# A hybrid DeltaNet and attention trunk: its first layer begun on half the tokens, the second layer's modulation sums moved to another stage, and the attention mask taken into the scan

## The chip, the cores and the metric

One Trainium2 chip, one core of it. The metric is the device time of one execution in microseconds (us), the median of several runs. The engines are named as the profile does: PE (TensorE, the matmuls), DVE (VectorE), ACT (ScalarE), POOL (GpSimd) and SP (SyncE, whose queue issues the transfers).

## The reference

Two layers on 1024 tokens of width 1024, all in float32. Both get six vectors of 1024 values each (shift, scale and gate for the mixer and for the FFN) from one conditioning vector. Layer one's mixer is a gated DeltaNet with 8 heads, layer two's is stick-breaking attention with 16 heads of width 64; each is followed by a SwiGLU FFN of inner width 2816.

```python
def reference(x, c, ada_w, ada_b, ...):
    cond = silu(c)
    for i in range(2):
        mod = cond @ ada_w[i] + ada_b[i]                    # 6 * 1024 values
        sh1, sc1, gt1, sh2, sc2, gt2 = split(mod, 6)
        h = rms_norm(x, norm1_g[i]) * (1 + sc1) + sh1
        y = gated_deltanet_mixer(h, ...) if i == 0 else stick_breaking_mixer(h, ...)
        x = x + gt1 * y
        h = rms_norm(x, norm2_g[i]) * (1 + sc2) + sh2
        x = x + gt2 * ((silu(h @ gate_w) * (h @ up_w)) @ down_w)
    return x

# stick-breaking attention, for a block of 128 queries and all keys up to it
z = q @ k.T * scale
causal = s_pos < t_pos                                      # strictly below the diagonal
log_1m = where(causal, log_sigmoid(-z), 0)
log_stick = cumsum(log_1m, reverse=True) - log_1m
a = where(causal, exp(log_sigmoid(z) + log_stick), 0)
o = a @ v
```

## The kernel before

The activations lie transposed: x is 8 tiles of 128 features by 1024 tokens (`xs[k]`), and a half c of the tokens is 512 of them. Each large product is done as three matmuls of 128 x 512 in a reduced format (`mm3`, L269, L271, L273): the high part of the weights (`wh`) by the high part of the activations, `wh` by their low part, and the low part of the weights (`wl`) by the high part. Both weight parts are made as the weights arrive, `wh` by a cast on ACT (L263) and `wl` by a subtraction on DVE (L264); `slab` loads 128 x 512 weights and splits them. The normed input `h` is split in the same way.

There are five stages.

1. **Start.** x is loaded half after half (`load_x`). For each half ACT squares it, DVE adds the squares up (L329), PE sums over the features (`norm_scale`, L333), and DVE multiplies x by the result (L1525). Then eight blocks of 1 MB of the modulation weights are loaded (`first_mods`); PE multiplies each by the conditioning vector (L97, L101) and `place_mods` puts two columns each into `mod` (L228, L229). That is shift and scale of the first mixer. `make_gsc` (L365) and `norm_part` (L342 to L346) then make `h` for both halves.
2. **DeltaNet.** Eight heads go through stages a to d, merged round by round (`t` from -2 to 6). `stage_a(0)` computes q and k of head 0 for the first half and then for the second, then the small products for the gates a and b (L743), then v. The other 32 column blocks of layer one's modulation are spread over the rounds as units of `row_steps` on PE (L97, L101, ended by L205), by a table of counts.
3. **FFN0.** `ffn(0)` walks over 22 column blocks f. The FFN's products are arranged as a fast matrix multiplication with seven products in place of eight, so DVE has many additions (L463, L551 to L604) between them. For even f the two blocks of f before it are multiplied by the output weights (`out_gemm`). Beside it runs `side`, units of layer two's modulation (`mod_unit`): 256 KB is loaded for each half of a unit, scaled by the conditioning values, summed over 8 blocks of 128 x 128, and `mod_end` (L205) sums over the partitions on PE. 24 of the 48 units are done here, three for two values of f, in the form `spare`: ACT scales (L172) and POOL adds (L178 to L183).
4. **Attention.** `stickbreak.main` first makes the second half of h (`norm_h`), spills x to memory, and then `attention` runs head pairs: `qkv(pp + 1)` is merged with `attend(pp)` and three modulation units in the form with sums on DVE (L174 once and L176 seven times for a unit). Three units are left behind the seventh round. For a block of queries `scores` makes z for two heads on PE, sigmoids of z and of -z on ACT (L1425), a scan on DVE that multiplies the second up from right to left (L1429), and a product of both on DVE (L1431); `turned` transposes on PE (L1442) and copies on ACT (L1443), and `weigh` multiplies by v. The mask is added to z on the diagonal block by two matmuls with `mask_b` (L1421, in the trace under L97).
5. **FFN1**, the same as FFN0 without `side`.

The order on every engine's queue is fixed when the program is built: a list scheduler takes instructions in the order of the code, and `merge` interleaves generators by the costs that they yield.

## Time and profile before

| | |
|---|---|
| median of three runs | 2895.55 us (2890.51 to 2895.74) |
| the profiled execution | 2890.06 us, its span 2888.4 us |
| PE | 2716.4 us busy, 94% |
| DVE | 2033.9 us, 70% |
| ACT | 1381.7 us, 48% |
| POOL | 95.1 us, 3% |
| transfers | 214 MB, 74 GB/s over the span |

The granted clock of PE was 0.98 of full speed over the span. The stages lie at about 0 to 59 us (start), 59 to 700 (DeltaNet), 700 to 900 (output products and the first part of FFN0), 900 to 1490 (FFN0), 1490 to 2105 (attention), and 2105 to 2888 (output products and FFN1). Busy shares are averages over these stages; what an edit is worth is read from its own stage.

### The profile page before, as it was taken

How to read it: one execution, taken by the hardware profiler on the slowest of the kernel's cores; microseconds unless marked ns; L12 is line 12 of the kernel's file. 1: busy time of each engine (PE TensorE's matmuls, PEld its weight loads, DVE VectorE, ACT ScalarE, POOL GpSimd, SP SyncE). 2: the span in 40 equal slices, each digit the busy share in tenths (PEclk: the TensorE clock that was granted, in tenths of full speed). 3: DMA queues.
4: the chain of work that ended last, by engine and by line, in shares of the span. 5: the costliest groups of instructions: out<-in, count | busy, mean ns of one | idle time of the engine just before them, and what ended most of it. 6: DMA issues, size and time to landing. Idle time of an engine off the chain costs nothing.

```text
span 2888.4 us, 40153 instructions
## 1 busy us (share of the span) xinstructions
PE 2716.4 (94%) x15202; PEld 2161.4 (75%) x15202; DVE 2033.9 (70%) x3352; ACT 1381.7 (48%) x2920; POOL 95.1 (3%) x174
## 2 busy tenths in 40 slices
PE   4999999998989999999999999999898999999999
PEld 2777777776767888778877666667576788888887
DVE  5777666666696666667786777677858866667666
ACT  5455555555453333433246777777845323223232
POOL 0000000001000111110000000000000000000000
PEclk9999999998999999999999999999899999999999
DMA  6312222234112222222231111111321111111113
GB/s 218 108 56 83 80 76 72 80 103 144 59 37 70 80 70 81 70 82 78 61 110 66 51 52 52 48 52 52 132 66 55 46 57 55 52 54 49 55 56 102
DMA packets 136288, 214.22 MB, mean 74 GB/s; under 512 B 33696, under 2 KB 62240, under 8 KB 136096
## 3 DMA queue, kind: packets, MB, share of 16 engines
q1 hardware_dynamic: 136096, 211.66, 23.1%
q8 instruction: 120, 1.97, 0.3%
q14 instruction: 72, 0.59, 0.1%
HBM read 195.75 MB, written 15.86 MB: 73 GB/s over the span
## 4 chain that ended last, share of the span: by engine, by line
PE 67%; DVE 15%; ACT 12%; DMA 3%; issue 3%; POOL 1%; SPq 0%; ACTq 0%; POOLq 0%; DVEq 0%
PE m L269 9%; PE m L273 8%; PE m L271 8%; PE s L273 6%; PE s L269 6%; PE s L271 5%; PE g L273 5%; PE g L269 5%; PE g L271 5%; DVE S L1429 2%; PE m L97 2%; DMA ada<-in_ada_w_dram 2%; ACT S L1425 2%; DVE wl L264 1%; PE s L97 1%
## 5 line engine op out<-in xcount | busy, mean ns | idle before, releaser
L269 PE MATMUL m<-h,wh 128*128 128x512 f32 x904 | 360.9, 408 | 7.3 <-DVE X L371 5.1
L273 PE MATMUL m<-h,wl 128*128 128x512 f32 x904 | 350.7, 397 | 10.6 <-DVE wl L264 10.6
L271 PE MATMUL m<-h,wh 128*128 128x512 f32 x904 | 351.1, 397 | 0.3 <-DVE h L359 0.3
L269 PE MATMUL g<-h,wh 128*128 128x512 f32 x856 | 313.4, 407 | 22.8 <-ACT wh L263 20.0
L273 PE MATMUL g<-h,wl 128*128 128x512 f32 x856 | 308.4, 401 | 13.0 <-DVE wl L264 13.0
L371 DVE SCALAR_TENSOR_TENSOR X<-m,mod,X 128x512 f32<-128x512 f32 x224 | 166.8, 750 | 209.7 <-PE m L273 209.6
L271 PE MATMUL g<-h,wh 128*128 128x512 f32 x856 | 303.1, 398 | 0.8 <-DVE h L447 0.8
L263 ACT CAST wh<-ga 128x512 fp32r<-128x512 f32 x168 | 100.7, 621 | 291.6 <-PE s L271 142.1
L273 PEld LDWEIGHTS m<-h,wl 128*128 128x128 f32 x904 | 172.5, 191 | 47.6 <-DVE wl L264 12.3
L269 PEld LDWEIGHTS m<-h,wh 128*128 128x128 f32 x904 | 171.7, 190 | 47.3 <-DVE X L371 8.0
L269 PEld LDWEIGHTS g<-h,wh 128*128 128x128 f32 x856 | 157.6, 190 | 58.8 <-ACT wh L263 25.8
L273 PEld LDWEIGHTS g<-h,wl 128*128 128x128 f32 x856 | 160.4, 190 | 52.9 <-DVE wl L264 20.9
L271 PEld LDWEIGHTS m<-h,wh 128*128 128x128 f32 x904 | 172.6, 191 | 34.5 <-DVE h L359 1.4
L1429 DVE TENSOR_TENSOR_SCAN S<-S,sbc 128x256 f32<-128x256 f32 (+7 forms) x128 | 170.0, 1348 | 33.0 <-ACT S L1425 32.9
L271 PEld LDWEIGHTS g<-h,wh 128*128 128x128 f32 x856 | 160.3, 190 | 33.2 <-DVE h L447 1.1
L263 ACT CAST wh<-wr 128x512 fp32r<-128x512 f32 x170 | 105.1, 625 | 146.4 <-PE m L271 74.3
L1425 ACT ACTIVATE S<-g,rq 128x512 f32<-128x512 f32 (+5 forms) x258 | 140.7, 596 | 37.2 <-DVE X L1431 15.3
L264 DVE TENSOR_TENSOR wl<-wr,wh 128x512 fp32r<-128x512 f32 x170 | 115.7, 684 | 52.0 <-ACT wh L263 51.9
L371 DVE SCALAR_TENSOR_TENSOR X<-s,mod,X 128x512 f32<-128x512 f32 x192 | 142.8, 744 | 13.1 <-PE s L273 13.0
L273 PE MATMUL s<-E,wl 128*128 128x512 f32 x352 | 137.7, 392 | 4.2 <-DVE wl L264 4.2
L269 PE MATMUL m<-S,wh 128*128 128x512 f32 x352 | 138.5, 394 | 0.0
L269 PE MATMUL s<-E,wh 128*128 128x512 f32 x352 | 138.2, 393 | 0.0
(454 smaller groups left out, 6040.4 us busy)
## 6 DMA issues: line engine op xcount, KB each, us to landing
ada<-in_ada_w_dram SPq DMA_DIRECT2D x160, 256.0 KB, 2.6
wo<-in_ffn_wo_dram SPq DMA_DIRECT2D x96, 256.0 KB, 2.8
ua<-in_ffn_wi_dram SPq DMA_DIRECT2D x88, 256.0 KB, 2.6
ga<-in_ffn_wi_dram SPq DMA_DIRECT2D x42, 512.0 KB, 3.6
wr<-in_dn_w_dram SPq DMA_DIRECT2D x68, 256.0 KB, 2.9
wr<-in_sb_w_dram SPq DMA_DIRECT2D x54, 256.0 KB, 2.7
E<-in_ada_w_dram SPq DMA_DIRECT2D x8, 1024.0 KB, 10.1
wr<-in_dn_wo_dram SPq DMA_DIRECT2D x24, 256.0 KB, 2.6
```

What stands on the lines that cost most here:

```text
L97: ins = f()
L263: S.copy(out=hi[:, :w], in_=raw[:, :w])
L264: V.tensor_tensor(out=lo[:, :w], in0=raw[:, :w], in1=hi[:, :w].bitcast(F32), op=ALU.subtract)
L269: PE.matmul(o, lhsT=wh, rhs=mh, start=start, stop=False)
L271: PE.matmul(o, lhsT=wh, rhs=ml, start=False, stop=False)
L273: PE.matmul(o, lhsT=wl, rhs=mh, start=False, stop=stop)
L371: V.scalar_tensor_tensor(out=xs[k][:, cs], in0=ps, scalar=mod[:, layer, 24 * which + 16 + k:24 * which + 17 + k], in1=xs[k][:, cs], op0=AL ...
L1425: S.activation(out=o[hd][:, tk], in_=z[:, hd, 0:wb], func=AF.Sigmoid, scale=rq[:, c, i, hd:hd + 1])
L1429: V.tensor_tensor_scan(pw[:, 0:w][:, ::-1], pw[:, 0:w][:, ::-1], zero_b.to_broadcast((P, w)), 1.0, op0=ALU.mult, op1=ALU.add)
```

## The change

- x is loaded half by half: `fetch_x(0)`, the squares and the norm of that half, the eight blocks of `first_mods`, the first two weight slabs of q (`there`), then `fetch_x(1)`. `stage_a(0)` does q and k for the first half of the tokens, then calls `second`, which norms the second half and makes its h, and then does the second half.
- The counts of layer one's units in DeltaNet's rounds are 4 4 3 3 3 3 3 3 6 in place of 3 3 4 4 4 4 4 3 3.
- Of layer two's 48 units 40 run in FFN0 (five for two values of f) with the sums on DVE, with a single buffer for the loaded half, and 8 in attention, one in a round and one behind the seventh.
- `stickbreak.main` hands the second half's norm and the spill of x to `attention` as a generator (`second`, the letter n in the order string `od0`), and `qkv(0)` takes its steps between its products.
- The mask matmuls are gone. The scan's second operand is now a real tile `late`, 0 and, on and above the diagonal, 1, with maximum in place of addition, so that the running product is 1 there. Behind `turned` POOL sets the diagonal block of the transposed weights to zero where the mask is (64 selections of 128 x 256).

```diff
+    def slabs(src):
+        return [slab(src[:, half * HALF:(half + 1) * HALF], 4) for half in range(2)]
...
                 next(side, None)
+                next(side, None)
                 if f % 2 == 0:
...
-    def deltanet(h, after):
+    def deltanet(h, after, there, second):
...
+            if hh == 0:
+                pre = [big(), big()]
+                for c in range(2):
+                    if c:
+                        second()
+                    for i in range(2):
+                        yield from gemm_steps([pre[i][:, c, :]], [c], dn_w[i * NH + hh], h,
+                                              there=None if c or i else there)
...
-            add(islice(mg, (3, 3, 4, 4, 4, 4, 4, 3, 3)[t + 2]), 'oM')
+            add(islice(mg, (4, 4, 3, 3, 3, 3, 3, 3, 6)[t + 2]), 'oM')
...
-            run(norm_h(h, 1, 0, 1, accs[0], ("S4", "S6")))
-            spill_x()
-            attention(h, after)
+            def second():
+                for _ in norm_h(h, 1, 0, 1, accs[0], ("S4", "S2")):
+                    yield 1.0
+                spill_x()
+            attention(h, after, second())
...
+        late = cp.tile([P, T], mybir.dt.bfloat16, tag="eye16", name="late")
+        G.memset(late[:, 0:T - P], 0.0)
...
+        V.tensor_copy(late[:, T - P:], late_f)
...
-            od0 = '012a435bNNdeyTNNy'
+            od0 = '0n1nnnnnnnnnr24a35bNNdeyTNNy'
...
-                if b == nb - 1:
-                    for hd in range(2):
-                        made.append(partial(PE.matmul, z[:, hd, wb - P:wb], lhsT=ident_b, rhs=dmask, start=False,
-                                            stop=True))
...
-                V.tensor_tensor_scan(pw[:, 0:w][:, ::-1], pw[:, 0:w][:, ::-1], zero_b.to_broadcast((P, w)), 1.0,
-                                     op0=ALU.mult, op1=ALU.add)
+                V.tensor_tensor_scan(pw[:, 0:w][:, ::-1], pw[:, 0:w][:, ::-1], late[:, T - w:T][:, ::-1], 1.0,
+                                     op0=ALU.mult, op1=ALU.max)
...
+            own = aT[i // 4][:, :, i % 4, ts_]
+            G.affine_select(out=own, in_=own, pattern=[[0, 2], [1, P]], compare_op=ALU.is_gt, fill=0.0, base=0,
+                            channel_multiplier=-1)
...
-        mg = mod_steps(1, range(24, 48))
+        mg = mod_steps(1, range(40, 48))
         run(qkv(0))
         for t in range(SBP - 1):
-            merge([attend(t), qkv(t + 1), islice(mg, 3)], [56.448, 40.2, 40.5])
+            merge([attend(t), qkv(t + 1), islice(mg, 1)], [56.448, 40.2, 40.5])
...
+    fetch_x(0)
+    load_x(0, range(KT))
     for q in range(KT):
         rows.append(first_mods(0, q))
...
-        todo.append(ffn(0, mod_steps(1, range(24), spare=True)))
+        todo.append(ffn(0, mod_steps(1, range(40))))
...
+        there = slabs(dn_w[0])
+        fetch_x(1)
+        def half_h(c):
+            for k in range(KT):
+                norm_part(h, 0, 0, c, k, xs[k][:, c * HALF:(c + 1) * HALF], k % 2 == 1)
+        def second():
+            load_x(1, range(KT), ("S2", "S0"))
+            half_h(1)
```

The order on PE at the very start of the kernel before (names with numbers are buffers; `m_136` and `m_172` are the two norm sums, `E_...` the modulation blocks):

```order
L333 MATMUL m_136<-S_5_110,onesf 128x512
L333 MATMUL m_172<-S_5_110,onesf 128x512
L101 MATMUL m_187<-E_10_185,sc_c 32x256
L97 MATMUL m_187<-E_10_185,sc_c 32x256 x7
L101 MATMUL m_200<-E_13_198,sc_c 32x256
L97 MATMUL m_200<-E_13_198,sc_c 32x256 x7
L228 MATMUL s_211<-cT,row_196 128x1 x2
```

And on PE in the changed kernel, where the first half's products of q and k end (L336 is the norm sum, `adac` and `ada` belong to units of `row_steps`, L748 are the gate products, called L743 before):

```order
L271 MATMUL g_427<-h_323,wh_487 128x512
L273 MATMUL g_427<-h_315,wl_488 128x512
L336 MATMUL m_520<-S_5_110,onesf 128x512
L205 MATMUL m_593<-cT,adac_453 128x1
L101 MATMUL m_596<-ada_597,sc_c 32x128
L97 MATMUL m_596<-ada_597,sc_c 32x128 x3
L97 MATMUL m_596<-ada_599,sc_c 32x128 x4
L748 MATMUL m_653<-h_308,S_116_649 32x512
```

The second norm sum has moved from in front of the modulation products to behind the first half's q and k.

The order on DVE in FFN0 before, at the end of an even f (L588 to L604 combine the seven products; `wl_9386` and `wl_9403` are the first low weights of the next f):

```order
L588 TENSOR_TENSOR S_1622_9101<-m_9315,S_1609_9039 128x512
L589 TENSOR_TENSOR S_1609_9039<-g_9083,S_1609_9039 128x512
L463 TENSOR_TENSOR s_1683_9424<-ga_9381,ua_9420 128x512
L595 TENSOR_TENSOR S_1622_9101<-s_9335,S_1622_9101 128x512
L264 TENSOR_TENSOR wl_9386<-ga_9381,wh_9385 128x512
L596 TENSOR_TENSOR S_1622_9101<-g_9083,S_1622_9101 128x512
L597 TENSOR_TENSOR S_1609_9039<-S_1622_9101,S_1609_9039 128x512
L602 TENSOR_TENSOR S_1609_9039<-m_9355,S_1609_9039 128x512
L264 TENSOR_TENSOR wl_9403<-ga_9381,wh_9402 128x512
```

The same place on DVE in the changed kernel (`adac` and `ada` are the modulation unit; lines are three or so higher):

```order
L591 TENSOR_TENSOR S_1603_8955<-m_9007,S_1590_8893 128x512
L174 TENSOR_SCALAR adac_8990<-ada_8991,sc_c 128x128
L592 TENSOR_TENSOR S_1590_8893<-g_8937,S_1590_8893 128x512
L176 SCALAR_TENSOR_TENSOR adac_8990<-ada_8991,sc_c,adac_8990 128x128
L598 TENSOR_TENSOR S_1603_8955<-s_9027,S_1603_8955 128x512
L176 SCALAR_TENSOR_TENSOR adac_8990<-ada_8991,sc_c,adac_8990 128x128
L599 TENSOR_TENSOR S_1603_8955<-g_8937,S_1603_8955 128x512
L176 SCALAR_TENSOR_TENSOR adac_8990<-ada_8991,sc_c,adac_8990 128x128
L600 TENSOR_TENSOR S_1590_8893<-S_1603_8955,S_1590_8893 128x512
L605 TENSOR_TENSOR S_1590_8893<-m_9047,S_1590_8893 128x512
L264 TENSOR_TENSOR wl_9078<-ga_9073,wh_9077 128x512
```

Four of the unit's eight sums stand between the additions, and the next f's first `wl` has moved behind L605, the addition that takes the last product.

## Rows read from the trace of the kernel before

**Rows 1.** The page's part 4, the chain that ended last: share by engine.

```profile
PE 67%; DVE 15%; ACT 12%; DMA 3%; issue 3%; POOL 1%; SPq 0%; ACTq 0%; POOLq 0%; DVEq 0%
```

**Rows 2.** Timeline, start: us, duration, engine, line, operation, count, idle before it and releaser.

```profile
25.61 2.08 PE L333 MATMUL m<-S,onesf 128*128 128x512 f32 x2 [9.61 <-DVE S L329]
...
44.22 0.16 DVE L229 TENSOR_TENSOR mod<-s,sc_c 128x2 f32<-128x2 f32 x1 [1.02 <-PE s L228]
...
58.72 0.80 PE L269 MATMUL g<-h,wh 128*128 128x512 f32 x1 [13.97 <-ACT wh L263]
...
83.09 7.56 PE L743 MATMUL m<-h,S 128*32 128x512 f32 x32
...
92.30 0.71 PE L269 MATMUL g<-h,wh 128*128 128x512 f32 x2
```

**Rows 3.** Window: length, engines' busy us (instructions), PEclk, DMA share, GB/s.

```profile
2.00:31.50 29.50, 7.94 (x38) 2.71 (x39) 18.24 (x36) 15.34 (x26) 1.10 (x7) 1.00 0.97 357
```

**Rows 4.** Window in DeltaNet's first rounds: PE, PEld, DVE, ACT, POOL.

```profile
120.00:140.00 20.00, 15.39 (x125) 12.48 (x126) 19.58 (x42) 8.70 (x20) 0.00 (x0) 0.91 0.46 131
```

**Rows 5.** Timeline, PE: one unit of layer one's modulation among the v products.

```profile
105.26 0.28 PE L205 MATMUL m<-cT,adac 128*128 128x1 f32 x2
...
106.04 0.72 PE L269 MATMUL g<-h,wh 128*128 128x512 f32 x2
```

**Rows 6.** One line, L585 on ACT, in FFN0 and in FFN1: durations, first and last start.

```profile
L585 ACT ACTIVATE S<-S x17: 632/633/636, 868.1 to 1367.2; 128x512 f32<-128x512 f32 x17
...
L585 ACT ACTIVATE S<-S x17: 632/633/634, 2267.4 to 2749.5; 128x512 f32<-128x512 f32 x17
```

**Rows 7.** Timeline, PE: the ending of a unit in FFN0 among the products.

```profile
916.82 0.39 PE L273 MATMUL s<-E,wl 128*128 128x512 f32 x1
917.05 0.28 PE L205 MATMUL m<-one,adac 128*128 128x1 f32 x2
...
917.50 0.40 PE L271 MATMUL m<-E,wh 128*128 128x512 f32 x1
```

**Rows 8.** Window in FFN0, and from its waits: us, times, longest.

```profile
905.00:1350.00 445.00, 437.82 (x1930) 357.12 (x1929) 305.06 (x484) 171.36 (x373) 66.12 (x105) 1.00 0.25 76
...
PE g L273 <- DVE wl L264: 4.2, 8, 0.6
```

**Rows 9.** Groups by line: a modulation unit's sums on DVE (busy us, mean ns).

```profile
L176 DVE SCALAR_TENSOR_TENSOR adac<-ada,sc_c,adac 128x128 f32<-128x128 f32 x168 | 58.6, 349 | 11.3 <-DMA ada<-in_ada_w_dram 7.7
L174 DVE TENSOR_SCALAR adac<-ada,sc_c 128x128 f32<-128x128 f32 x24 | 6.6, 277 | 0.0
```

**Rows 10.** Waits in attention, 1570 to 2145 us; and its units by form.

```profile
DVE adac L176 <- DMA ada<-in_ada_w_dram: 6.0, 7, 3.5
...
L174 DVE TENSOR_SCALAR adac<-ada,sc_c 128x128 f32<-128x128 f32 x22 | 6.1, 276 | 0.0
```

**Rows 11.** Groups by form: one subtraction on DVE, FFN0 (905 to 1350), FFN1 (2300 to 2745).

```profile
L463 DVE TENSOR_TENSOR S<-S,S 128x512 fp32r<-128x512 f32 x30 | 23.2, 775 | 12.8 <-ACT S L607 12.8
...
L463 DVE TENSOR_TENSOR S<-S,S 128x512 fp32r<-128x512 f32 x31 | 21.2, 684 | 0.0
```

**Rows 12.** Timeline, PE: the second norm sum at attention's start.

```profile
1511.80 2.07 PE L333 MATMUL m<-S,onesf 128*128 128x512 f32 x2 [4.63 <-DVE S L329]
```

**Rows 13.** Window of one attention round; timeline of two mask products.

```profile
1694.49:1766.53 72.04, 66.23 (x420) 49.61 (x419) 50.71 (x76) 56.22 (x107) 0.00 (x0) 1.00 0.16 52
...
1747.37 0.28 PE L97 MATMUL g<-mask_b 128*128 128x128 bf16 x2
1747.47 0.48 PE L269 MATMUL m<-h,wh 128*128 128x512 f32 x1
```

**Rows 14.** Groups by line: a selection on POOL; the scan on DVE.

```profile
L699 POOL TENSOR_SCALAR_AFFINE_SELECT S<-S 128x128 f32<-128x128 f32 x1 | 0.3, 343 | 0.0
...
L1429 DVE TENSOR_TENSOR_SCAN S<-S,sbc 128x256 f32<-128x256 f32 (+7 forms) x128 | 170.0, 1348 | 33.0 <-ACT S L1425 32.9
```

**Rows 15.** Timeline behind the seventh round: DVE and PE.

```profile
2052.95 1.51 DVE L176 SCALAR_TENSOR_TENSOR adac<-ada,sc_c,adac 128x128 f32<-128x128 f32 x4 [3.48 <-DMA ada<-in_ada_w_dram]
...
2069.85 2.91 PE L1442 MATMUL s<-ident,X 128*128 128x128 f32 x12 [2.48 <-ACT E L1443]
```

68 lines of the change are left out of this document (33 added, 35 removed).

## The prediction

> **What bounds the kernel now.** I read the chain of work that ended last first: 67% of it is TensorE (PE), 15% VectorE (DVE) and 12% ScalarE [rows 1]; the busy shares of the table say the same. So a change can win in three ways only: fill the stretches where PE stands idle, take instructions off PE, or shorten the waits of PE. The timeline and the windows show where PE is idle: the first 58 us, the front of DeltaNet where DVE is full, small gaps in each attention round, and the end of attention. The two FFNs are the control: FFN1 runs the same products as FFN0 without any modulation beside them.
>
> **Start: x in halves (first part of the change).** Before, PE's queue holds the norm sum of the second half of x ahead of the first modulation products; it runs at 25.61 us after 9.61 us of idleness [rows 2], and only then do the eight modulation blocks follow, about 2.1 us apart, up to the last modulation on DVE at 44.22 us [rows 2]. In the change the eight 1 MB blocks are loaded right behind the first half of x. The transfers move 357 GB/s from 2 to 31.5 us [rows 3], which is 29.5 x 0.357 = 10.5 MB, just the 2.1 MB of half an x and the 8.4 MB of blocks. So the last block lands near 31.5 us. Behind a block's landing I take 2.4 us for its products, its copy and its add (one block's pitch before and a little more), which puts the last modulation at 33.9 us: 10.3 us sooner. The first product began at 58.72 us [rows 2], 14.5 us behind the modulations: it waited for the cast of its weight slab, which stood on ScalarE behind nearly all casts of both halves of h. In the order of the change that slab is cast ahead of h, so the first product can follow in 2.4 us, near 36.3 us: 22.4 us sooner. Not all of this is kept. The q and k products of the first half are 48 matmuls of 0.23 us, the pitch of such matmuls [rows 7], 11 us; I let them end near 51.5 us, four us later than that, because h comes chunk by chunk from ScalarE and PE has stood idle before. Then PE takes the second norm sum, about 2 us [rows 2], and must wait until DVE and ScalarE have made the scale and the second half of h; from the eight DVE multiplications and the first cast I allow 6 us until the first piece is there, and the rest arrives at the pace of the products. The 32 products of a and b (7.56 us) stand in the same stretch. That leads to the v products near 77 us in place of 92.30 us [rows 2], a gain of about 15 us. Behind this DVE is the bound: it is busy for 19.58 of the 20 us from 120 on, while PE is busy for 15.39 [rows 4]. DVE's own work for head 0 can begin sooner by the same time, so most of the gain passes through. I take **-13 us**, bounds -16 and -8 (half of it lost in that stretch).
>
> **Row units of layer 0.** A unit holds PE from 105.26 to 106.04 us, 0.78 us [rows 5]. Five of them go from the middle rounds, where PE is nearly full, to the first two rounds and the last, where PE has idle time. All of it gained is 5 x 0.78 = 3.9 us; some of the ends is not idle. **-2 us**, bounds -4 and -1.
>
> **FFN0.** Two values of f make a pair of steps, the period in which the products repeat. ScalarE's silu of the same kind stands at 868.1 and 1367.2 us, eight pairs apart in FFN0, and at 2267.4 and 2749.5 us in FFN1 [rows 6]: 62.39 us a pair against 60.26. FFN0 pays 2.13 us a pair for its three modulation units. One ending of a unit (L205) costs PE about 0.22 us: a matmul at 916.82 has 0.23 us to itself, while from the ending at 917.05, with one matmul behind it, it is 0.45 us to the next at 917.50 [rows 7]. Three are 0.66 us; 1.47 us is left for waits, of which the waits for wl alone are 4.2 us in 445 us [rows 8]. After it there are five units a pair: 1.10 us for the endings. The sums leave ScalarE and GpSimd and go to DVE: one scaling of 277 ns and seven multiply-adds of 349 ns [rows 9], 2.72 us a unit, 13.6 us a pair. DVE is busy for 305.06 of 445 us there [rows 8], 42.8 us a pair, so it comes to 56.4 us of some 62.8 us, 90%. That covers the work by 6.4 us a pair, and no more: the order shows the first wl of the next f now behind the addition that waits for the last product (L605), where it stood ahead of it before, so PE meets a wait of about 1 us there in each f; against that ScalarE loses 8 scalings a unit, and its casts come sooner. A unit also has one buffer of half its size, and its next half is fetched only when the four sums have ended; in attention, where this scheme runs now, DVE waits 6.0 us in all for that data, 7 times in 22 units [rows 10]. I take the waits at 1.4 us, as now: 60.26 + 1.10 + 1.4 = 62.76 us, 0.37 us a pair more, **+3 us** over eight pairs. If casts and products get easier to 0.4 us of waits it is -5 us; if each f pays 1.5 us (3.05 us a pair) it is +16 us. I stay near the middle, since rows on DVE at 90% do not exist in this trace.
>
> One row on GpSimd leaving: the subtraction of two SBUF tiles takes 775 ns in FFN0 and 684 ns in FFN1 [rows 11], 30 of them in 445 us: 0.09 x 30 / 7.1 pairs, 0.4 us of DVE a pair, which is inside the bounds.
>
> **Attention, start.** The first products no longer stand behind the whole second norm in the code. In PE's order the second norm sum comes after one product of the first half instead of before it, and PE waited 4.63 us for it [rows 12]; DVE's sums, for which it waits, are the same and DVE is full there. **-1 us**, bounds -3 and 0.
>
> **Attention, the seven rounds.** A round takes 72.04 us, PE is busy for 66.23 and DVE for 50.71 [rows 13]. Gone are 128 mask products: two of them hold PE from 1747.37 to 1747.47 us [rows 13], so 64 pairs cost 64 x 0.11 = 7 us. Gone are 16 of the 24 endings of units, 16 x 0.22 = 3.5 us, and with 14 of the 21 units of the rounds 14 x 2.72 = 38 us of DVE [rows 9]. PE's share alone is 7 + 3.5 = 10.5 us; part of it only widens the idle 5.8 us of a round, since the tails of the cycle sigmoid, scan, multiplication, transposition set the pace in a few places. New are 64 selections on GpSimd of 128 x 256 elements between the copy and the weighing products. The nearest row is a 128 x 128 one of 343 ns [rows 14]; between the same and double it is 0.34 to 0.69 us. The weighing product stands a scores step behind its last copy, so I cost them at nothing; if that cover were gone, half of the 64 (one in each pair of blocks is the late one) would cost 32 x 0.69 = 22 us at the most. The scan keeps its form and length with a true second operand for a repeated one; its rows are 170.0 us in all [rows 14]; at nothing, and at 5% either way 8.5 us of DVE, mostly idle-covered. **-8 us**, bounds -14 and +3.
>
> **Attention, end.** Three units were run behind the seventh round, at the time when DVE leads the chain: it stood 3.48 us for their data, and PE waited 2.48 us for a tile behind [rows 15]. One unit is left. **-4 us**, bounds -6 and -2.
>
> **The sum.** -13 - 2 + 3 - 1 - 8 - 4 = -25 us. The profiled execution took 2890.06 us, 5.5 us under the median of the runs shown, 2895.55. From the first it is 2865, from the second 2870.5; I take **2868 us** between them.
>
> **Rivals.** *VectorE becomes the bound in FFN0* (slower). If each of the ten half units of a pair makes DVE wait x us for its transfer, a pair takes 56.4 + 10x us: it binds from x = 0.64, and from x = 0.95 (65.9 us) the whole gain of 25 us is gone. For it: data waits of up to 3.48 us [rows 15] happen already where units stand close. Against: the mean wait per half is 6.0 / 44 = 0.14 us in attention [rows 10]. At x = 1.3 a pair takes 69.4 us, 6.6 us more than forecast, 53 us in all: 2921 us. *The start's gain is given back*: DVE, full from 120 to 140 us [rows 4], has no earlier work to take, and the wait for the second half is longer than I allow; 3 us of 13 stay: 2878 us. *The selections disturb the scans*: GpSimd's selection and DVE's scan and multiplication meet, each of the 64 holds DVE for 0.34 to 0.69 us, 64 x 0.5 = 32 us, 40% of it in the tails where DVE leads: +13 us, the body ends at +5 in place of -8: 2881 us. For it: the lengthened subtractions beside GpSimd's additions [rows 11]. Against: DVE has 21 us free in a round.
> The Trainium skill (SBUF — State Buffer, section Who interferes with whom) has this as a rule that speaks against the change: an operation of DVE with two SBUF inputs contends with a GpSimd instruction that reads SBUF, and one of them blocks for the whole instruction of the other. The trace agrees where GpSimd works, 775 against 684 ns [rows 11]; no run here shows it on a scan. By the rule in full the time would be that of the rival of the selections.
> *It moves costs about and no more*: FFN0 pays 16 us in place of 3 and the start keeps 5 of 13, with the rest as forecast less 2: 2868 + 13 + 8 + 2 = 2891 us, within 0.2% of before.
>
> **How the numbers follow.** Forecast 65%, start given back 12%, selections 10%, costs moved 6%, VectorE bound 7%. Faster by over 0.2% (5.8 us, about what can be told from no change): 65 + 12 + 10 = 87%; within 0.2%: 6%; slower: 7%. The bounds of the terms add to -48 and +8 us; all ends together are unlikely, so below I go to 2846 (-22 from the forecast), above to 2890, which takes in the start and the selections and leaves out the last two cases and a little of the low end.
>
> **What would show it.** In the changed profile: the last modulation near 34 us, the first product near 36, the v products near 77; the FFN0 silu rows 62 to 63.5 us a pair, with DVE near 90% busy; rounds of attention of about 71 us and no PE wait for GpSimd; scans of unchanged length; no DVE wait of 3 us for modulation data at the end of attention. A pair over 65 us, scans longer by a tenth, or v products behind 88 us would prove the forecast wrong.

## The result

The changed kernel takes 2907.64 us (median of seven runs), the kernel before 2894.05 us in the runs beside it: ratio 1.0055, 95% interval 1.0037 to 1.0072, some 16 us slower (13.6 us between the two medians). Forecast were 25 us less. The profiled execution has a span of 2909.1 us against 2888.4. In that execution of the kernel before, the first product comes early, at 58.72 us; in the ten later runs with the same start it comes at 59.77 to 63.53 us. Against one of those the differences in the table below would be one to five us smaller.

The page of the changed kernel, parts 1 and 4 (busy time, share and count of each engine; the chain that ended last), answers to [rows 1]:

```profile
PE 2729.1 (94%) x15074; PEld 2168.8 (75%) x15074; DVE 2086.1 (72%) x3543; ACT 1319.8 (45%) x2722; POOL 58.8 (2%) x118
...
PE 69%; DVE 17%; ACT 8%; DMA 3%; issue 3%; SPq 0%; ACTq 0%; DVEq 0%
```

PE has 128 instructions less and is busy for longer. The page doesn't say where; a list of landmarks on the timeline does. Each is the start of one instruction that both kernels have.

| landmark | before | after | difference |
|---|---|---|---|
| modulations of the first mixer ready (make_gsc) | 44.41 | 43.84 | -0.6 |
| first product | 58.72 | 45.41 | -13.3 |
| head 0's v convolution (ACT) | 105.46 | 100.80 | -4.7 |
| head 1's k convolution | 143.59 | 143.54 | 0.0 |
| head 1's v convolution | 154.29 | 157.13 | +2.8 |
| head 2's q convolution | 187.25 | 204.93 | +17.7 |
| head 7's v convolution | 613.38 | 620.81 | +7.4 |
| first output product of DeltaNet | 696.47 | 725.04 | +28.6 |
| FFN0, silu of f = 2 | 868.10 | 892.35 | +24.3 |
| FFN0, silu of f = 18 | 1367.17 | 1407.57 | +40.4 |
| attention's first scan | 1572.93 | 1616.60 | +43.7 |
| first scan of the seventh round | 2000.20 | 2026.70 | +26.5 |
| FFN1, silu of f = 2 | 2267.40 | 2289.33 | +21.9 |

So there are two losses in DeltaNet (first rounds, and between the last round and the output product) and one in FFN0, and one gain, larger than forecast, in attention's rounds. Windows in DeltaNet show idle PE (columns as in [rows 4]; the column behind the engines is the granted clock):

```profile
100.00:120.00 20.00, 14.25 (x93) 10.57 (x91) 8.95 (x16) 12.76 (x39) 0.74 (x1) 0.74 0.50 132
...
140.00:160.00 20.00, 15.42 (x72) 12.25 (x70) 18.70 (x31) 8.60 (x24) 0.52 (x1) 0.97 0.18 63
160.00:180.00 20.00, 16.22 (x173) 13.36 (x173) 9.52 (x11) 6.44 (x24) 0.74 (x1) 0.60 0.13 41
...
700.00:730.00 30.00, 16.74 (x97) 12.35 (x97) 14.83 (x35) 14.44 (x38) 0.00 (x0) 0.60 0.64 202
```

PE works 14.25 of 20, 31.64 of 40 and 16.74 of 30 us there, part of it at the lower of its two rates (granted 0.74, 0.60 and 0.60 on the mean), beside stretches in which it stood still. The first of these gaps is made up again, for head 1's k convolution is not late. The lasting loss of the first rounds lies between head 1's v and head 2's q convolution, so in the second. In the gaps from 100 and from 700 us, and behind 160 us, no engine is full, so PE waits for something in a queue. The timeline of the changed kernel gives PE's waits, and the transfer queue of SP beside them (start and duration in us, engine, line, operation; in brackets the wait ahead and what ended it):

```profile
76.35 27.62 SPq L193 DMA_DIRECT2D ada<-in_ada_w_dram  x4
...
105.02 0.39 SPq L257 DMA_DIRECT2D wr<-in_dn_w_dram  x1
...
109.68 1.22 PE L269 MATMUL g<-h,wh 128*128 128x512 f32 x2 [3.52 <-ACT wh L263]
...
138.03 7.04 SPq L193 DMA_DIRECT2D ada<-in_ada_w_dram  x3
...
155.27 0.61 PE L273 MATMUL g<-h,wl 128*128 128x512 f32 x2
160.54 0.36 PE L101 MATMUL m<-dd,S 64*64 64x64 f32 x1 [4.66 <-DVE dd L1047]
...
167.18 0.38 SPq L257 DMA_DIRECT2D wr<-in_dn_w_dram  x1
...
174.66 0.73 PE L269 MATMUL g<-h,wh 128*128 128x512 f32 x2 [1.68 <-ACT wh L263]
...
701.03 2.75 SPq L193 DMA_DIRECT2D ada<-in_ada_w_dram  x3
...
706.18 2.41 SPq L386 DMA_DIRECT2D yr<-ydn  x3
...
725.04 1.22 PE L269 MATMUL m<-h,wh 128*128 128x512 f32 x2 [2.71 <-ACT wh L263]
```

From 76 to 104 us SP's queue is in the loads of four half units of layer one's modulation (L193); the next weights of DeltaNet (L257) are issued at 105.02, and PE waits for their cast until 109.68. From 138 us more half units follow, and the next weights are asked for at 167.18. PE's last product with weights ends at 155.88, and the next comes at 174.66; between them PE has only the small products of a head, which wait for DVE, and those of a unit. At the end the last three of these loads stand at 701 to 704 us, and only at 706 come the loads of `yr`, the input of the output product. Units and weights share three buffers (`wr`). So the waits of SP's queue in the changed kernel name L97 on PE, the products of the unit before, as releaser (total us, times, longest), from 60 to 180 us:

```profile
SPq L193 <- PE m L97: 45.2, 3, 21.7
```

That gave theory A, that the added units stand ahead of the weights in SP's queue, with the halved start as its rival for the first rounds (theory B).

### The profile page after: what moved, and what is told of

Same layout as the page of the kernel before. It is cut to its first block, busy times and chain, and to the rows that moved or that the text cites. A ratio compares the mean times of both kernels' runs of the same rounds, so it can differ in the third digit from the quotient of the medians.

```text
span 2909.1 us, 39773 instructions
## 1 busy us (share of the span) xinstructions
PE 2729.1 (94%) x15074; PEld 2168.8 (75%) x15074; DVE 2086.1 (72%) x3543; ACT 1319.8 (45%) x2722; POOL 58.8 (2%) x118
## 4 chain that ended last, share of the span: by engine, by line
PE 69%; DVE 17%; ACT 8%; DMA 3%; issue 3%; SPq 0%; ACTq 0%; DVEq 0%
PE m L269 10%; PE m L273 9%; PE m L271 9%; PE s L269 5%; PE s L273 5%; PE s L271 5%; PE g L269 5%; PE g L271 5%; PE g L273 4%; PE m L97 2%; DVE wl L264 2%; PE s L1464 1%; DVE S L1451 1%; ACT S L1446 1%; PE s L97 1%
## 5 line engine op out<-in xcount | busy, mean ns | idle before, releaser
L273 PE MATMUL g<-h,wl 128*128 128x512 f32 x856 | 312.4, 403 | 17.7 <-DVE wl L264 17.5
L1451 DVE TENSOR_TENSOR_SCAN S<-S,late 128x256 f32<-128x256 f32 (+7 forms) x128 | 171.5, 1361 | 70.0 <-ACT S L1446 70.0
L263 ACT CAST wh<-wo 128x512 fp32r<-128x512 f32 x96 | 59.7, 622 | 198.4 <-PE s L271 97.3
```

Of the source, the lines that this page charges most:

```text
L263: S.copy(out=hi[:, :w], in_=raw[:, :w])
L273: PE.matmul(o, lhsT=wl, rhs=mh, start=False, stop=stop)
L1451: V.tensor_tensor_scan(pw[:, 0:w][:, ::-1], pw[:, 0:w][:, ::-1], late[:, T - w:T][:, ::-1], 1.0, op0=ALU.mult, op1=ALU.max)
```

## Experiments on DeltaNet's counts and the start

Edits are given against the kernel before, or against the changed kernel where it says so. All ratios are to runs of the kernel before beside them, whose median lay between 2894 and 2897 us.

**e1: the counts undone** (on the changed kernel).

```diff
-            add(islice(mg, (4, 4, 3, 3, 3, 3, 3, 3, 6)[t + 2]), 'oM')
+            add(islice(mg, (3, 3, 4, 4, 4, 4, 4, 3, 3)[t + 2]), 'oM')
```

> The changed kernel with one line undone: layer one's modulation units go over DeltaNet's rounds as 3 3 4 4 4 4 4 3 3 again. Theory A (queue): the four units in the first rounds and the six in the last take the three buffers that the weights use too; SP's queue stands at their loads and the next weights stand behind. That costs about 17 us by head 2's first convolution and about 21 us between the last round and the first output product, against 5 us won in the middle. Undone, the first output product comes near 695 us instead of 725, and the time falls by 25 to 33 us, to about 2880 us, below the kernel before. Theory B (halved start): the loss of the first rounds belongs to the halved start, and only the last round is cured: 17 us less and 5 us of the middle lost again, about 2895 us, with head 2's first convolution still near 205 us.

2888.4 us, ratio 0.9974 (0.9964 to 0.9984): 19 us below the changed kernel and 8 us below the one before. Head 2's q convolution comes at 187.91 us, the first output product at 698.86. Windows of e1:

```profile
100.00:120.00 20.00, 19.41 (x144) 14.56 (x143) 11.88 (x25) 14.42 (x46) 0.74 (x1) 1.00 0.49 132
120.00:140.00 20.00, 14.11 (x84) 11.08 (x84) 18.70 (x38) 6.92 (x13) 0.00 (x0) 0.74 0.51 147
...
160.00:180.00 20.00, 19.88 (x230) 16.08 (x230) 9.41 (x12) 9.09 (x30) 0.52 (x1) 1.00 0.17 53
...
700.00:730.00 30.00, 28.95 (x144) 23.50 (x143) 21.60 (x42) 16.28 (x36) 0.00 (x0) 1.00 0.45 150
```

And the timeline of e1 in the first rounds and at DeltaNet's end (start, duration, engine and line):

```profile
77.20 3.50 SPq L193 DMA_DIRECT2D ada<-in_ada_w_dram  x2
82.58 0.33 SPq L257 DMA_DIRECT2D wr<-in_dn_w_dram  x1
87.05 17.62 SPq L193 DMA_DIRECT2D ada<-in_ada_w_dram  x2
...
158.88 0.50 PE L273 MATMUL g<-h,wl 128*128 128x512 f32 x1
...
658.12 9.26 SPq L386 DMA_DIRECT2D yr<-ydn  x3
...
687.16 1.38 SPq L257 DMA_DIRECT2D wr<-in_dn_wo_dram  x2
...
698.86 0.48 PE L269 MATMUL m<-h,wh 128*128 128x512 f32 x1
```

PE is full from 160 to 180 and from 700 to 730 us at the granted clock 1.00. The gap from 100 us has only moved: from 120 to 140 us PE works 14.11 us at 0.74, so that gap is not the loss. In e1 a load of weights stands at 82.58 us between the units, and from 80 to 140 us the queue asks for weights seven times, in the changed kernel six times; so e1 still has products with weights to put between the small ones behind 157 us (158.88). At the end `yr` is asked for at 658 us in place of 706, and the output weights at 687 us, where the changed kernel asks at 721. SP's wait by itself does not tell the two apart, for from 60 to 180 us e1 has nearly as much of it:

```profile
SPq L193 <- PE m L97: 37.3, 3, 17.7
```

What counts is which loads stand behind it. Theory A holds for both places; B falls. The time gained, 19 us by the medians, is less than the 25 to 33 us expected.

**e2: the counts alone.** The one line of e1 the other way round, on the kernel before.

> The kernel before with only the counts 4 4 3 3 3 3 3 3 6. Theory A: both losses appear without any other edit, first output product near 725 us instead of 696, 25 to 33 us slower, about 2923 us. Theory B: the first rounds stay as before (head 2's first convolution near 187 us), the last round costs about 17 us and the middle gives 5: about 2906 us.

2921.67 us, ratio 1.0086 (1.0069 to 1.0103): 25 us slower without any other edit. Head 2's q convolution at 210.74 us, first output product at 728.72. Both losses are the counts'.

**e3: the halved start alone**: `fetch_x`, `there`, `second` in `deltanet` and `half_h` as in the diff, and nothing else.

> The kernel before with only the halved start (x in halves, q and k of the first half of the tokens first). Theory A: the halved start keeps the 4.7 us that it wins by head 0's last convolution (100.8 us against 105.5), about 2889 us. Theory B: it loses some 12 us in the first rounds, head 2's first convolution near 205 us instead of 187, about 2906 us. In both the modulation blocks take about 3.4 us each on PE instead of 2.15, because PE stays at its lower rate through the start.

2891.96 us, ratio 0.9981 (0.9972 to 0.9991), 5 us faster, where 13 were forecast. Head 0's v convolution comes at 100.93 us, head 2's q convolution at 187.84. The modulation blocks take 3.4 us each, as in the changed kernel.

**e9: six units at the end alone.**

```diff
-            add(islice(mg, (3, 3, 4, 4, 4, 4, 4, 3, 3)[t + 2]), 'oM')
+            add(islice(mg, (3, 3, 4, 4, 4, 3, 3, 2, 6)[t + 2]), 'oM')
```

> The kernel before with counts 3 3 4 4 4 3 3 2 6: the first rounds untouched, six units in the last. If the six units alone hold the weight buffers in front of the first output product, head 2's first convolution stays near 190 us while that product comes 18 to 22 us later than before, behind a last round otherwise equal: 15 to 20 us slower, about 2913 us. If both places need each other (the queue stays behind from the first rounds on), it is within 5 us of before.

2912.17 us, ratio 1.0051 (1.0028 to 1.0074). Head 2's convolution is not late (189.15 us), the first output product comes at 720.15. The six units cost 15 us (by the ratio) to 18 us (by the medians) by themselves; the queue need not be behind before.

## Experiments on the modulation in FFN0

The step of a pair of f values, as in [rows 6] (L588 is the silu, L585 in kernels with the old numbering), is read from the group of these silus (count, durations, first and last start). First the changed kernel:

```profile
L588 ACT ACTIVATE S<-S x17: 632/633/635, 892.4 to 1407.6; 128x512 f32<-128x512 f32 x17
```

The same group in e4:

```profile
L585 ACT ACTIVATE S<-S x17: 632/633/636, 870.8 to 1389.2; 128x512 f32<-128x512 f32 x17
```

And in e11:

```profile
L585 ACT ACTIVATE S<-S x17: 632/633/635, 871.6 to 1359.3; 128x512 f32<-128x512 f32 x17
```

An eighth of the stretch from first to last is 64.40, 64.80 and 60.96 us; before it was 62.39.

**e4: the moved modulation alone.**

```diff
+                next(side, None)
...
-        todo.append(ffn(0, mod_steps(1, range(24), spare=True)))
+        todo.append(ffn(0, mod_steps(1, range(40))))
...
-            merge([attend(t), qkv(t + 1), islice(mg, 3)], [56.448, 40.2, 40.5])
+            merge([attend(t), qkv(t + 1), islice(mg, 1)], [56.448, 40.2, 40.5])
```

> The kernel before with only layer two's modulation moved: 40 units in FFN0 with sums on VectorE, 8 in attention. If the units themselves make FFN0 slower, the pair of steps takes 64.4 us as in the changed kernel (62.4 before), 16 us in all; attention's rounds shrink from 72.0 us to 70.5 to 71, 7 to 10 us in all, its end by 3 us: about 2897 to 2900 us. If the cost of FFN0 came from somewhere else in the change, the pair stays near 62.7 us and the time is about 2886 us.

2902.38 us, ratio 1.0024 (1.0014 to 1.0033): 7 us slower, near the first value expected. FFN0 loses 19 us by this edit alone; five rounds of attention take 358.98 us against 362.07, 0.6 us a round.

**e10: forty units in the old form** (on e4).

```diff
-        todo.append(ffn(0, mod_steps(1, range(40))))
+        todo.append(ffn(0, mod_steps(1, range(40), spare=True)))
```

> The kernel before with 40 units in FFN0 and 8 in attention, but FFN0's in the old form: ScalarE scales, GpSimd adds. VectorE keeps its old load there. If VectorE's load makes FFN0 slower, the pair of steps takes 62.4 + 2 x 0.22 = 62.8 us; if the number of units does it (the one buffer, the transfers in the queue, the endings), it takes 64 us or more also here.

2960.46 us, ratio 1.0225 (1.0195 to 1.0255); the pair takes 71.2 us. That is the side of the number of units in what was expected, but it does not show them as the cause in e4: this form itself does not carry five units, and PE waits 25.3 us in 425 us for casts on ScalarE, which now stand among the scalings.

**e11: the old 24 units, summed on VectorE.**

```diff
-        todo.append(ffn(0, mod_steps(1, range(24), spare=True)))
+        todo.append(ffn(0, mod_steps(1, range(24))))
```

> The kernel before with the same 24 units in FFN0 and 24 in attention, but FFN0's sums on VectorE instead of ScalarE and GpSimd. If VectorE's load is the cause, the pair of steps takes between 62.4 and 64.4 us, near 63.3 by its share (three fifths); if ScalarE's and GpSimd's work was the hindrance before, it falls below 62.

2877.91 us, ratio 0.9942 (0.9919 to 0.9964), 17 us faster than before by one argument. A window of 425 us in FFN0, of e11:

```profile
915.00:1340.00 425.00, 425.00 (x1895) 352.24 (x1894) 340.17 (x641) 117.77 (x197) 0.00 (x0) 1.00 0.26 79
```

The same window of e4:

```profile
915.00:1340.00 425.00, 407.62 (x1792) 330.00 (x1792) 343.22 (x715) 109.75 (x183) 0.00 (x0) 1.00 0.29 90
```

With 24 units PE has no idle time at all; the pair is FFN1's 60.26 us and three endings, 0.66. With 40, at nearly the same busy time of DVE (343 against 340 us, 81% where 90% was forecast), PE stands 17.4 us. DVE's mean load does not tell the two apart, and the old form on ScalarE and GpSimd was itself the hindrance before. Among PE's waits in e4 is the one that the prediction named (total us, times, longest):

```profile
PE g L273 <- DVE wl L264: 11.8, 7, 1.7
```

**e13: that wait taken away.** On e4, the split of each f's first weights gets a high priority, so that its low part stands ahead of the closing additions.

```diff
-            product(b1, ga[:, 0], b11)
+            product(b1, ga[:, 0], b11, True)
...
+            if early:
+                with tc.high_priority():
+                    hi, lo = split_slab(w, HALF)
```

> Forty units in FFN0 as in the run with the moved modulation alone (2902 us, pair of steps 64.8 us), but the split of each f's first weights gets a high priority, so that its low part stands ahead of the closing additions of the f before on VectorE's queue, as it does with 24 units. Theory O (order): the two us a pair are PE's wait for that low part behind the additions; the pair falls to 61.5 to 62.3 us and the time to 2880 to 2885 us. Theory L (load): VectorE is too full with 40 units, whatever the order; the pair stays at 64 us or more and the time within 5 us of 2902.

2908.54 us, ratio 1.0045 (1.0031 to 1.0059), pair 64.9 us. The wait is gone (1.3 us in 420 us) and others stand in its place: for the unit's sums before an ending (3.3 us), for casts on ScalarE (2.4 us). They are smaller: PE stands 9.4 us in 420 where it stood 17.4 in 425, and yet the pair is no shorter, since PE is busy for longer in each; why is open. Theory O falls.

**e14: 32 units**, two in an odd f, two in an even one; 16 in attention.

```diff
                 next(side, None)
+                if f % 2:
+                    next(side, None)
...
-            merge([attend(t), qkv(t + 1), islice(mg, 3)], [56.448, 40.2, 40.5])
+            merge([attend(t), qkv(t + 1), islice(mg, 2)], [56.448, 40.2, 40.5])
...
-        todo.append(ffn(0, mod_steps(1, range(24), spare=True)))
+        todo.append(ffn(0, mod_steps(1, range(32))))
```

> 32 units in FFN0 (four a pair of steps) on VectorE and 16 in attention. In its order the next f's first low weights stand behind the additions in every second f, as with 40 units. Theory O: the stall is nearly that of 40 units, pair 63.5 to 64.5 us. Theory L: the load lies halfway between 24 (60.96 us) and 40 units (64.8 us), pair near 62 us, or lower still where VectorE has slack.

2905.55 us, ratio 1.0039 (1.0026 to 1.0052), pair 64.8 us, the whole loss of 40 units at 78% of DVE. So it is a step, not a slope, near what theory O said of this run, though e13 spoke against O's reason. The silus one by one tell where it lies: an odd f takes 23.2 us on the mean against 19.3 in e11, an even f 41.6 in both. So it is the second unit in an odd f that costs here. In e4 the odd f takes 22.0 us and the even one, with three units, 42.8.

**e15: forty units, one in an odd f and four between the output products of an even one** (on e4).

```diff
-                next(side, None)
                 if f % 2 == 0:
                     for m in range(0, KT, 2):
                         out_gemm(f - 2, gt[f - 2:f], [0, 1], m)
-                    next(side, None)
+                        if m < 6:
+                            next(side, None)
```

> Forty units in FFN0 on VectorE as in the run with the moved modulation alone, but spread: one unit in an odd f, which has no output products, and four between the output products of an even f (before: two and three). In FFN1 VectorE has 4.7 us free in the 19.1 us of an odd f and 13.9 us free in the 40.7 us of an even one; a unit takes 2.7 us. Theory P (place): two units do not fit an odd f, and the wait of PE for the next weights at its end is the loss; spread so, the pair takes 60.3 + 1.1 = 61.4 to 61.9 us in place of 64.8, and the time falls by 23 to 27 us, to about 2878 us. Theory L (load or number of units): the pair stays above 63.5 us and the time near 2900 us.

2935.04 us, ratio 1.0136 (1.0122 to 1.015), pair 68.7 us: some 57 us above what theory P expected, and 35 above theory L. Its waits in 420 us (us, times, longest):

```profile
DVE adac L176 <- DMA ada<-in_ada_w_dram: 26.4, 19, 2.8
...
PE m L205 <- DVE adac L176: 15.6, 12, 2.2
```

The odd f is cured (19.2 us), and the even one takes 49.5. Four units in a row wait for one another: each half is fetched into the one buffer only when the half before it is summed, DVE stands meanwhile with all that is queued behind, and PE stands before the ending (L205). **e16** is the changed kernel with e1's line, this spread in FFN0 and attention's norm in one piece (e8's edit).

> The changed kernel with the three repairs: layer one's old counts in DeltaNet, the forty units spread as one and four, and attention's second norm in one piece. If theory P holds, it is 24 us faster than the changed kernel with its counts undone (2888 us), about 2862 us, and faster than the version with 24 units (2870 us), because attention's rounds take 69.4 us in place of 72 with one unit in each. If theory L holds, about 2886 us.

2914.85 us, ratio 1.0059 (1.0047 to 1.0071). Both values expected, 2862 and 2886 us, were missed: the pair takes 68.5 us, as in e15.

**e17: the buffer's wait shortened** (on e4): a unit comes in four quarters into the two halves of its buffer in turn.

```diff
-        for half in range(2):
+        for half in range(4):
...
+            a = ring[0][:, 2 * (half % 2):2 * (half % 2) + 2]
-            SY.dma_start(out=a, in_=ada_w[layer, j, :, 4 * half:4 * half + 4, :])
+            SY.dma_start(out=a, in_=ada_w[layer, j, :, 2 * half:2 * half + 2, :])
```

> Forty units in FFN0 as in the run with the moved modulation alone, placed as there, but a unit is loaded in four quarters into the two halves of its one buffer in turn, so that the next quarter is fetched while the last is summed (twice the transfers, half as long). Theory U (buffer): the sums of two units in succession wait for one another's data and hold VectorE's queue, and PE behind it; the pair falls from 64.8 to 62 us or less, the time to 2885 us or less. If the buffer is not the cause (VectorE waited for data only 8.4 us in 425 us), the pair stays at 64 us or more, the time at 2900 to 2910 us.

2897.58 us, ratio 1.0008 (0.9998 to 1.0017); pair 63.75 us. That is 1.05 us a pair better than e4, about a third of its 3.4 us above what 24 units plus two endings would take (60.96 + 0.44). It lies between the two values expected, and outside what one and the same form shows from run to run (64.40 to 64.89 us in e4, e1 and the changed kernel). The single buffer is part of the cause. What holds the rest stays open: it is neither the place of the weights alone (e13) nor the mean load (e14); that with two units close together some wait of DVE reaches PE, whichever, is argued, not shown.

## Experiments on attention

**e5: attention's edits alone** (mask in scan, selections, second norm as steps).

> The kernel before with only attention's two edits: the mask in the scan and on GpSimd, and the second norm as steps of the first head pair. If the terms of the change add up (start -5, counts +25, modulation +6, the whole about +14), this one is worth -9 to -13 us: about 2885 us. Rounds of attention take 69.5 to 70 us in place of 72.4 (the mask products and the waits around them), the first scan comes 2 to 3 us later behind FFN0 than before. If the short rounds of the changed kernel come from the fewer modulation units instead, rounds stay at 71.5 to 72 us and the time is within 3 us of before.

2892.9 us, ratio 0.9992 (0.9983 to 1.0001): no more than 3 us, against 9 to 13 expected. The window of rounds two to six, in the kernel before:

```profile
1638.13:2000.20 362.07, 335.63 (x2091) 250.97 (x2092) 253.57 (x378) 281.40 (x533) 0.00 (x0) 0.99 0.16 52
```

In e5:

```profile
1640.94:1998.88 357.94, 337.28 (x2011) 251.04 (x2011) 257.97 (x378) 281.59 (x531) 23.20 (x41) 0.97 0.17 52
```

In e4:

```profile
1661.84:2020.82 358.98, 329.25 (x2072) 245.87 (x2071) 228.76 (x287) 280.16 (x532) 0.00 (x0) 1.00 0.12 37
```

In the changed kernel:

```profile
1679.74:2026.70 346.96, 327.93 (x1991) 247.24 (x1991) 233.18 (x287) 274.76 (x526) 24.37 (x41) 0.98 0.12 39
```

A round takes 72.4, 71.6, 71.8 and 69.4 us. Each edit alone brings 0.8 and 0.6 us, both together 3.0. In e5 PE does fewer instructions in no less busy time (337.28 against 335.63 us) at a granted clock of 0.97 in place of 0.99, though it stands still less (20.7 us in the window against 26.4). So part of the saving is given back as longer busy time; what lowered the clock is not shown. Only with DVE relieved as well (233 us busy against 258) do the rounds get clearly shorter; that the chain of sigmoid, scan and transposition is then what shortens is argued, not shown.

**e6: start and attention together; e7: the same with PE warmed up; e8: start and mask without the norm as steps.** e7 puts 18 unused products ahead of the first norm sum; e8 undoes `second` in `stickbreak`, so that the norm is in one piece again.

```diff
+    together([partial(PE.matmul, wps, lhsT=onesf, rhs=warm, start=True, stop=True) for _ in range(18)])
```

The edit of e8, on e6:

```diff
-            def second():
-                for _ in norm_h(h, 1, 0, 1, accs[0], ("S4", "S2")):
-                    yield 1.0
-                spill_x()
...
-            attention(h, after, second())
+            run(norm_h(h, 1, 0, 1, accs[0], ("S4", "S6")))
+            spill_x()
+            attention(h, after, iter(()))
...
-            od0 = '0n1nnnnnnnnnr24a35bNNdeyTNNy'
+            od0 = 'r012a435bNNdeyTNNy'
```

> The halved start and attention's two edits on the kernel before, without the counts and without the moved modulation: the parts that paid alone. If they add up: -5 and -9 to -13, about 2880 us, 0.5% below before and below the changed kernel with its counts undone (2888). If the start's gain is eaten by DeltaNet's first rounds, about 2886 us.

2885.85 us, ratio 0.9971 (0.996 to 0.9981). That is the second value expected (2886), but for another reason: e3 and e5 alone measured -5 and -2 us, and these add up to it. What had been put too high was attention's part.

> The same with 18 idle products of 128 x 512 on PE ahead of the first norm sum (their result is not used), so that PE has worked without a pause before the modulation blocks come. If the halved start lost its 9 us because PE stood at its lower rate, the blocks now take 2.15 to 2.6 us each instead of 3.4, the last modulation comes near 34 us instead of 43 and the first product near 37 instead of 45.4. If DeltaNet's first rounds follow PE, 5 to 9 us less than the kernel without them, about 2873 us; if VectorE bounds those rounds, head 0's convolutions come sooner but head 2's stay near 188 us and the time is the same within 2 us.

2892.49 us, ratio 0.9982 (0.9968 to 0.9995). The experiment missed: the products kept PE until 20.47 us, 6 us beyond the sum's old time, then, behind one block at the high rate, PE stood 4.46 us for the norm's scale, and the next blocks were at the low rate again. The last modulation came at 46 us. It tells nothing of the rate itself.

> The halved start and the mask edit alone: the second norm of attention stands again in front of the first products. If handing that norm out as steps cost time (the first scan came 2 to 3 us later behind FFN0), this one is 2 to 3 us faster than the kernel with both; if it is worth the forecast 1 us, 1 us slower.

2886.81 us, ratio 0.9971 (0.9959 to 0.9983), the same as e6 in time. From FFN0's last silu to the first scan it is 103.7 us in e8, 106.9 in e6 and 105.0 before, so the norm as steps costs some 3 us there (106.8 to 108.1 us in the five runs that have it with the new mask, 103.7 to 104.4 in the three without, e8, e12 and e16). In the medians of e6 and e8 this does not appear.

**e12: what paid, together**: halved start, mask edit, and e11's 24 units on VectorE; the old counts.

> The halved start, the mask edit, and layer two's 24 units of FFN0 on VectorE, with 24 in attention and the old counts in DeltaNet. If the parts add up (-0.58% from the 24 units alone, -0.29% from start and mask): 2870 us, 0.8 to 0.9% below the kernel before, below all others. If FFN0's gain and the rest overlap, 2876 us.

2869.59 us, ratio 0.9907 (0.9892 to 0.9921): 25 us below the kernel before and 38 below the changed one. FFN0's pair takes 60.8 us. The parts add up, as expected (2870).

## Why the prediction was wrong, point by point

- **Start: the sign right, the size wrong** (-13 forecast, -5 measured in e3). The failed step is the 2.4 us behind each block's landing. That was the pitch of a PE at its full rate, read from one execution, which ran the products of its last block in 0.40 us; the ten later runs with the same start ran them in 0.63 or 0.64. In the changed kernel the last block landed at 32.4 us, near the 31.5 forecast, but on PE the blocks came every 3.42 us, so PE and not the transfers set the end, and the modulations were ready at 43.84 us instead of 33.9. From the timeline of the changed kernel, a block and the first product:

```profile
28.42 1.01 PE L228 MATMUL s<-cT,row 128*128 128x1 f32 x4 [0.55 <-ACT row L221]
29.36 0.63 PE L101 MATMUL m<-E,sc_c 128*32 128x256 f32 x1
...
45.41 0.80 PE L269 MATMUL g<-h,wh 128*128 128x512 f32 x1 [2.30 <-ACT h L348]
```

  The same from e8, which has the same program at its start:

```profile
26.84 0.61 PE L228 MATMUL s<-cT,row 128*128 128x1 f32 x4 [0.55 <-ACT row L221]
27.44 0.38 PE L101 MATMUL m<-E,sc_c 128*32 128x256 f32 x1
...
39.14 0.80 PE L269 MATMUL g<-h,wh 128*128 128x512 f32 x1 [2.30 <-ACT h L348]
```

  The same matmul lasts 0.63 and 0.38 us, which I read as the lower and the higher of PE's two rates, 1.2 and 2.4 GHz, from the durations alone: the window's row gives a granted clock of 1.00 in both. In e8's last block, where the same product takes 0.61 to 0.63 us again, the row does give the lower one, 0.50:

```profile
31.60:45.00 13.40, 9.77 (x37) 6.83 (x38) 9.50 (x25) 9.27 (x18) 0.77 (x5) 0.50 0.77 263
```

  With six blocks at the higher rate the first product came at 39.14 us, near the 36.3 forecast, and e8's head 2 convolution at 180.34 instead of e6's 187.74, so what PE gains at the start does arrive there. But from head 0's v to head 2's q convolution the runs with the new start and the old counts take 85.5 to 87.4 us, those with the old start 81.7 to 83.3. Four to five us of the gain are given back in the stretch where DVE is full, so the rival that it is given back there was right in part.
- **Row units: wrong in sign** (-2 forecast, +25 measured in e2). The failed step costed a unit by its 0.78 us on PE alone. The middle rounds did get shorter, 75.6 us against 76.9, even more than that. But a unit's loads also stand in SP's queue and take two of the three buffers that the weights need. Four in each of the first rounds and six in the last put the next weights behind them. Neither queue nor buffer was in the sum, nor in a rival, and with 27 us between forecast and result this term alone outweighs the whole forecast gain.
- **FFN0: mis-sized.** +3 was taken, with bounds of -5 and +16; it was 8 x 2.0 = 16 us by the landmarks, and 19 in e4. The wait of PE for the low weights was named and is there, 1.7 us, but taking it away did not help (e13). The term that failed is the 1.4 us of waits taken "as now"; by e11 the waits with three units on DVE are nil and with four they are over 3 us, so no straight line between them held. The rival that DVE's data waits bind in FFN0 was described rightly in e15 only, where units stand close. The rival of moved costs, with a chance of 6%, had both sizes right, 16 us in FFN0 and 5 of the start's 13; it too had nothing for the counts.
- **Attention's rounds: the direction right, too small** (-8 forecast, about -19 by the landmarks over seven rounds). I counted PE's saved instructions and took part of them; the two edits together shortened the chain by more than either (e4, e5). The selections cost nothing on the way of PE, and no wait of PE for GpSimd shows in the changed kernel. The selections' group in the changed kernel (busy us, mean ns of one), answering to [rows 14]:

```profile
L1468 POOL TENSOR_SCALAR_AFFINE_SELECT E<-E 128x256 f32<-128x256 f32 x50 | 32.1, 643 | 534.0 <-ACT E L1465 534.0
```

  643 ns lies inside the 0.34 to 0.69 us taken. The groups of the longest and the shortest scans of the changed kernel, and the shortest in the kernel before (L1429):

```profile
L1451 DVE TENSOR_TENSOR_SCAN S<-S,late 128x1024 f32<-128x1024 f32 x14 | 31.3, 2279 | 6.7 <-ACT S L1446 6.7
...
L1451 DVE TENSOR_TENSOR_SCAN S<-S,late 128x128 f32<-128x128 f32 x14 | 7.3, 518 | 0.0
...
L1429 DVE TENSOR_TENSOR_SCAN S<-S,sbc 128x128 f32<-128x128 f32 x14 | 5.9, 418 | 0.0
```

  A scan over 1024 elements lasted 2279 ns in the kernel before as well, but no selection runs beside one. Seven of the sixteen scans over 128 elements begin while a selection runs, and these last 0.63 us in place of 0.41. By the prediction's own sign, scans longer by a tenth, it was wrong for these. In the windows above DVE is busy for 4.4 us more with the selections than without, in five rounds (257.97 against 253.57, and 233.18 against 228.76). So the rule of the Trainium skill (SBUF — State Buffer, section Who interferes with whom) that weighed against this edit does show, on instructions that begin inside a selection. It is about 0.1 us of DVE for each of the forty selections of those rounds, where the rival of the selections took 0.5, and the rounds got shorter all the same.
- **Attention's start and end.** The start cost 3 us instead of winning 1 (by the landmarks, and by those of e6 against e8: the norm as steps). The end won 3 us, where 4 were forecast.

The parts alone are -5 (start), +25 (counts), +7 (modulation) and -2 us (attention), +25 in all; the whole is +16, since modulation and attention's edits help each other in the rounds (3.0 us a round together against 0.6 + 0.8, over seven rounds some 11 us). e1, which is the whole without the counts, agrees: its parts alone add up to nothing, and it measured -8 us.

## What to carry to other kernels

Cost a moved step by every queue and buffer that it uses, not by the engine that computes it: read the transfer queue's own waits at the place where it will stand, and ask which load is issued behind it. A chain of work through one buffer was free here while its parts stood far apart, and dear by a step when they stood close. A price read while PE runs at its full rate need not hold at a place where it has been idle, nor in the next execution. And a wait that looks like the cause (SP's 45.2 us) has to be read in the kernel without the loss too.

## What the runs showed of the hardware

At the start PE's lower rate cost more than its pauses: a block took 3.42 us in place of 2.15, with pauses of half a microsecond in both. Executions of the same start differ by 6 us according to whether PE rose to its higher rate after the first block (e8, from 18.8 to 31.6 us) or stayed low past the first product at 45.0 to 45.9 us (the changed kernel, e1, e3, e6, e12, e16), though PE was doing the same work with the same pauses. What decides this was not settled; a run of unused products ahead (e7) left a pause of 4.46 us behind it, and the rate was low again after that. The sums on GpSimd and ScalarE, which looked free because both engines were mostly idle, had cost FFN0 1.4 us a pair. And DVE instructions that begin while a GpSimd selection runs took some 0.2 us longer: a scan over 128 elements 0.63 us in place of 0.41, a multiplication of 639 elements 1.03 in place of 0.80. One of 383 elements that begins in the last 0.1 us of a selection was no longer (0.56 us).
